# Weight blocks split in halves, and recurrence steps emitted once per weight block, in a projection kernel with three recurrences

## The chip, the cores and the metric

The kernel runs on one core of one Trainium2 chip. The metric is the device time of one execution in microseconds, median of three runs. TensorE (PE) does the matrix products, VectorE (DVE) and ScalarE (ACT) the elementwise work, GpSimd (POOL) some copies and fills, and SyncE (SP) issues the loads.

## The reference

A layer over 272 tokens (16 meta tokens and 256 real ones) with a model width of 2048, in float32. The tokens are normalised and multiplied by one wide matrix; the columns of the result feed three recurrent mixers (A, B and C), three gates, and two outer products:

```python
xn = rmsnorm(h, norm_g[l])
(a_q, a_f, a_i, a_z, b_q, b_k, b_v, b_o, b_ig, b_fg, b_z,
 c_r, c_k, c_v, c_wd, c_ad, c_z, g_a, g_b, g_c) = split_cols(xn @ w_in[l])
y_a = hgrn2_mixer(...)      # A: 8 heads of 128
y_b = mlstm_mixer(...)      # B: 4 heads of 128 x 256
y_c = rwkv7_mixer(...)      # C: 16 heads of 64, with a triangular solve per chunk of 64
merged = (jax.nn.sigmoid(g_a) * (y_a @ w_br[l, 0])
          + jax.nn.sigmoid(g_b) * (y_b @ w_br[l, 1])
          + jax.nn.sigmoid(g_c) * (y_c @ w_br[l, 2]))
h = h + merged @ w_out[l]
return rmsnorm(h, final_norm_g)[:, N_META:]
```

Each mixer is a recurrence over chunks of the sequence: elementwise work, small products, and a state that one chunk hands to the next.

## The kernel before

**Products.** Weights and activations are split into a high and a low part (`wh` and `wl`, `xH` and `xL`), and each product of the reference becomes three: high by high, low by high, high by low. The weights stream from memory in blocks of 512 KB: four pieces of 128 rows by 256 columns in the projections, two of 128 by 512 in the gates and the last product. `Stream.load` (line 343) sends a block to one of four `raw` buffers through SP's queue. `Stream.cut` (line 351) makes its two parts: one ACT cast of the whole block gives `wh`, and one DVE subtraction of the whole block gives `wl`; both have three buffers. `Stream.next` (line 367) hands out the oldest cut block and cuts ahead, so that three are ready or on the way.

**Projections.** `gemm` (line 390) makes 256 columns of the wide matrix at a time, from four blocks. In each block `unit` does 12 products for the first 128 columns and 12 for the second: 24 products per block. Results are read out of PSUM by `evac` when all four blocks are done.

**Recurrences beside them.** Each mixer's work for a group of heads is a generator (`c_scan`, `b_scan`, `a_scan`) that emits a few instructions and yields. `Order` decides how far each generator runs: it keeps a clock for PE, ACT and DVE and adds a price per instruction (for DVE 0.07 us and 1.05 ns per element, for ACT 0.12 us and 0.84 ns). `Order.pump` (line 87) runs every generator whose next step is ready by these clocks within a look-ahead: 3.5 us for a step without a product; for one that starts with a product 2.0 us in C's scans and 0.3 us in B's and A's. `gemm` calls `pump` after each `unit`, so after every 12 products; `rows_unit` (line 1347), for the gates, calls it after every third product of 512 columns. `Order.finish` (line 105) runs a generator to its end at once; it is called where the next group needs the place of the last one (C's at the next R projection, B's at the next head, A's at the next group). The framework then fixes the order of each engine's instructions at build time. The engines run them in that order.

**Stages.** To 38 us the tokens are normalised and transposed and the first columns made. To 717 us follow 47 projections with the recurrences of C (four groups), B (four heads) and A (four groups) beside them. Then come three gate branches (`gate_branch`) and the product with `w_out`. `x_again` (line 1415), after the last gate of the first branch, opens the pool `rows` and writes `late["rp"]`; by then all recurrences are over.

C's scan holds the longest chains: a substitution of 31 steps on DVE (`Ltmp` and `LV`, two instructions each), scratch transfers through memory (`scv`, `sct`, `Vm`, `VT`), and then five chunks with three dependent products each (`cX`, `UV`, `cS`).

Of the kernel before, what the change touches and what calls it, by code (L numbers as in the profile page):

```python
# [9 lines left out]
F32 = mybir.dt.float32  # L10
# [4 lines left out]
ALU = mybir.AluOpType  # L15
# [135 lines left out]
def kernel(  # L151
# [29 lines left out]
    od = Order()  # L181
    V = Priced(nc.vector, "dve", od, tc)
    S = Priced(nc.scalar, "act", od, tc)
# [148 lines left out]
    class Stream:  # L332
# [18 lines left out]
        def cut(self):  # L351
            if not self.raw:
                return
            raw, uk, m = self.raw.pop(0)
            if self.extra and len(self.todo) + len(self.raw) < len(self.extra):
                h, l = self.extra.pop(0)
            else:
                h = wts.tile([P, uk, max(m, 256)], F32R, name="wh", tag="wh", bufs=3)
                l = wts.tile([P, uk, max(m, 256)], F32R, name="wl", tag="wl", bufs=3)
            saved, od.ready = od.ready, 0.0  # L360
            S.copy(out=h[:, :, 0:m], in_=raw[:, :, 0:m])
            od.ready = 0.0
            V.tensor_tensor(out=l[:, :, 0:m], in0=raw[:, :, 0:m], in1=h[:, :, 0:m].bitcast(F32), op=ALU.subtract)
            od.ready = saved
            self.split.append((h, l))

        def next(self):
# [4 lines left out]
                self.load()  # L372
            return self.split.pop(0)

    ws = Stream()

    def unit(h, l, u, kts, ps, aH, aL, t0, n, js):
        for k in range(UK):
            kk = u * UK + k
            rh = aH[:, kk, t0:t0 + n]  # L380
            mm(ps, h[:, k, js], rh, start=kk == 0, stop=False)
            mm(ps, h[:, k, js], aL[:, kk, t0:t0 + n], start=False, stop=False)
            mm(ps, l[:, k, js], rh, start=False, stop=kk == kts - 1)

    def apart(f):
        saved, od.ready = od.ready, od.clk["pe"]
        f()
        od.ready = saved

    def gemm(m, aH, aL, kts, t0, n, evac):  # L390
        nt = m // P
        ps = [gps.tile([P, 512], F32, name="gp", tag="g") for _ in range(nt)]
        for u in range(kts // UK):
            h, l = ws.next()
            for j in range(nt):
                unit(h, l, u, kts, ps[j][:, 0:n], aH, aL, t0, n, slice(j * P, (j + 1) * P))
                od.pump()
        for j in range(nt):
            apart(lambda: evac(j, ps[j][:, 0:n]))

# [2 lines left out]
    def proj(c0, m, t0, evac, before=None, after=None):  # L403
        ws_src = win[:, :, c0:c0 + m]
        blocks.append((ws_src, KT, lambda: gemm(m, xH, xL, KT, t0, T - t0, evac), before, after))
# [927 lines left out]

    late = {}
    WB = 512
    TK = 2

# [222 lines left out]
    for u in range(KT // UK):  # L1562
        h, l = ws.next()
        unit(h, l, u, KT, gw[0][:, 0:T], xH, xL, 0, T, slice(0, P))
        h, l = ws.next()
# [103 lines left out]
    for n, (c0, m) in enumerate(outs):  # L1669
        ps = [gps.tile([P, 512], F32, name="gp", tag="g") for _ in range(2)]  # L1670
        us = KT * m // 1024
        if n < len(outs) - 1:
            for u in range(us):
                h, l = ws.next()
# [55 lines left out]
```

## Time and profile before

| | |
|---|---|
| median of 3 runs | 1229.77 us (1229.72 to 1230.2) |
| profiled execution, its own time | 1229.33 us |
| span of its instructions | 1227.6 us |
| granted TensorE clock | 0.998 |
| PE busy | 1208.1 us (98%) |
| DVE busy | 879.2 us (72%) |
| ACT busy | 665.0 us (54%) |

The span runs from the first to the last instruction of the program; 1.7 us of the profiled execution's time lie around it. Busy time of an engine is the time in which at least one of its instructions ran, and a PE that is busy to 98% may still be late in single places: products overlap by more than half of their modelled length, so the lost time is read from the distance of their starts.

### The profile page before, as it was taken

What the parts mean: (1) busy time and instruction counts of PE and PEld (TensorE: products, weight loads), DVE (VectorE), ACT (ScalarE), POOL (GpSimd) and SP (SyncE); (2) the same over time, 40 slices, a digit from 0 to 9 for tenths busy, and PEclk for the clock granted to TensorE, in tenths of its full rate; (3) what the DMA queues carried; (4) which work ended last, traced back from release to release, by engine and by line L of the source; (5) the groups of instructions that cost most, each with busy time, mean ns of one, the idle gap of its engine ahead of it and who ended that gap; (6) DMA issues with size and microseconds to landing.
All of it is one profiled execution on the core that took longest, in us unless ns stands there. A gap on an engine that the chain in (4) does not pass through costs nothing.

```text
span 1227.6 us, 23061 instructions
## 1 busy us (share of the span) xinstructions
PE 1208.1 (98%) x9224; PEld 1104.2 (90%) x9224; DVE 879.2 (72%) x1491; ACT 665.0 (54%) x1032; POOL 57.0 (5%) x167
## 2 busy tenths in 40 slices
PE   8999999999999999999999999999999999999997
PEld 8999999999999999999999988888888888888887
DVE  6688996697975889995889986644555565556554
ACT  6765455663445764766664657544444444445444
POOL 3100001000051000010000000000000000000000
PEclk9999999999999999999999999999999999999999
DMA  8645564465563554463554454666766676665663
GB/s 254 184 138 166 155 172 130 129 183 155 155 171 104 158 165 137 140 170 105 162 163 142 139 164 153 190 188 189 226 197 193 191 225 200 191 193 172 193 197 121
DMA packets 172996, 207.43 MB, mean 169 GB/s; under 512 B 22331, under 2 KB 127160, under 8 KB 172488
## 3 DMA queue, kind: packets, MB, share of 16 engines
q1 hardware_dynamic: 171688, 202.21, 56.2%
q0 software_dynamic: 880, 3.22, 0.8%
q8 instruction: 72, 1.18, 0.4%
q10 hardware_dynamic: 320, 0.53, 0.1%
q14 instruction: 36, 0.29, 0.1%
HBM read 202.19 MB, written 3.74 MB: 168 GB/s over the span
## 4 chain that ended last, share of the span: by engine, by line
PE 85%; DVE 9%; ACT 3%; issue 2%; POOL 0%; DVEq 0%; ACTq 0%; POOLq 0%
PE gp L186 76%; PE cbank L186 5%; DVE wl L127 3%; PE bank L186 3%; ACT wh L127 1%; DVE Ltmp L127 1%; PE cbank L193 1%; DVE LV L127 1%; PE bank L193 1%; DVE UV L127 0%; DVE aY L127 0%; ACT L127 0%; DVE BK L127 0%; DVE aW L127 0%; DVE SC L127 0%
## 5 line engine op out<-in xcount | busy, mean ns | idle before, releaser
L127 DVE TENSOR_TENSOR wl<-raw,wh 128x1024 fp32r<-128x1024 f32 (+1 forms) x370 | 449.3, 1215 | 243.6 <-ACT wh L127 242.2
L127 ACT CAST wh<-raw 128x1024 fp32r<-128x1024 f32 (+1 forms) x370 | 386.7, 1046 | 387.0 <-PE gp L186 352.4
L186 PE MATMUL gp<-xH,wh 128*128 128x272 f32 (+3 forms) x1552 | 448.1, 289 | 0.2 <-ACT xH L127 0.2
L186 PE MATMUL gp<-xH,wl 128*128 128x272 f32 (+3 forms) x1552 | 444.0, 286 | 1.6 <-DVE wl L127 1.6
L186 PE MATMUL gp<-xL,wh 128*128 128x272 f32 (+3 forms) x1552 | 443.8, 286 | 0.1
L186 PEld LDWEIGHTS gp<-xH,wl 128*128 128x128 f32 x1552 | 292.4, 188 | 2.9 <-DVE wl L127 2.6
L186 PEld LDWEIGHTS gp<-xH,wh 128*128 128x128 f32 x1552 | 292.5, 188 | 2.2 <-ACT xH L127 0.5
L186 PEld LDWEIGHTS gp<-xL,wh 128*128 128x128 f32 x1552 | 292.2, 188 | 0.9 <-DVE xL L127 0.3
L186 PE MATMUL gp<-wh,xH 128*128 128x512 f32 x384 | 150.6, 392 | 0.0
L186 PE MATMUL gp<-wh,xL 128*128 128x512 f32 x384 | 150.5, 392 | 0.0
L186 PE MATMUL gp<-wl,xH 128*128 128x512 f32 x384 | 150.3, 391 | 0.0
L186 PEld LDWEIGHTS gp<-wh,xL 128*128 128x128 f32 x384 | 72.1, 188 | 15.5
L186 PEld LDWEIGHTS gp<-wl,xH 128*128 128x128 f32 x384 | 72.2, 188 | 15.0
L186 PEld LDWEIGHTS gp<-wh,xH 128*128 128x128 f32 x384 | 72.1, 188 | 15.0
L186 PE MATMUL gp<-wh,mH 128*128 128x512 f32 (+1 forms) x144 | 51.1, 355 | 0.0
L186 PE MATMUL gp<-wh,mL 128*128 128x512 f32 (+1 forms) x144 | 50.9, 354 | 0.0
L186 PE MATMUL gp<-wl,mH 128*128 128x512 f32 (+1 forms) x144 | 50.9, 354 | 0.0
L127 DVE TENSOR_TENSOR LV<-LV,Ltmp 40x31 f32<-40x31 f32 (+15 forms) x124 | 41.0, 331 | 2.6
L127 DVE TENSOR_TENSOR Ltmp<-LU,LV 40x31 f32<-40x31 f32 (+15 forms) x124 | 41.1, 332 | 2.4
L186 PEld LDWEIGHTS gp<-wh,mL 128*128 128x128 f32 x144 | 27.2, 189 | 3.8
L186 PEld LDWEIGHTS gp<-wh,mH 128*128 128x128 f32 x144 | 27.2, 189 | 3.7
L186 PEld LDWEIGHTS gp<-wl,mH 128*128 128x128 f32 x144 | 27.2, 189 | 3.7
(420 smaller groups left out, 1476.0 us busy)
## 6 DMA issues: line engine op xcount, KB each, us to landing
raw<-in_w_in_dram SPq DMA_DIRECT2D x288, 512.0 KB, 3.7
raw<-in_w_br_dram SPq DMA_DIRECT2D x48, 512.0 KB, 4.2
raw<-in_w_out_dram SPq DMA_DIRECT2D x32, 512.0 KB, 3.6
hres<-in_x_dram POOLq DMA_DIRECT2D x2, 1024.0 KB, 5.9
xt<-in_x_dram SPq DMA_DIRECT2D x3, 512.0 KB, 5.0
raw<-in_w_in_dram SPq DMA_DIRECT2D x4, 256.0 KB
fg<-in_final_norm_g_dram POOLq DMA_DIRECT2D x1, 1024.0 KB, 5.1
scr<-SC SPq DMA_DIRECT2D x16, 40.0 KB, 1.7
```

The source lines that it names most:

```text
L127: r = f(*a, **k)
L186: nc.tensor.matmul(o, lhsT, rhs, start=start, stop=stop)
L193: nc.tensor.transpose(o, a, i)
```

## The change

A block of full size (1024 elements per partition) is cut in two halves of 512, each with its own ACT cast and its own DVE subtraction, until `late["rp"]` exists; smaller blocks, and those after it, are cut whole. In `gemm`, `pump` is called after both units of a block, so after 24 products and no longer after 12. `late = {}` stands earlier in the file, as `cut` reads it.

```diff
             saved, od.ready = od.ready, 0.0
-            S.copy(out=h[:, :, 0:m], in_=raw[:, :, 0:m])
-            od.ready = 0.0
-            V.tensor_tensor(out=l[:, :, 0:m], in0=raw[:, :, 0:m], in1=h[:, :, 0:m].bitcast(F32), op=ALU.subtract)
+
+            n = 1 if uk * m < 1024 or "rp" in late else 2
+            for i in range(n):
+                us = slice(i * uk // n, (i + 1) * uk // n)
+                od.ready = 0.0
+                S.copy(out=h[:, us, 0:m], in_=raw[:, us, 0:m])
+                od.ready = 0.0
+                V.tensor_tensor(out=l[:, us, 0:m], in0=raw[:, us, 0:m], in1=h[:, us, 0:m].bitcast(F32), op=ALU.subtract)
             od.ready = saved
             self.split.append((h, l))
...
+    late = {}
     ws = Stream()
...
             h, l = ws.next()
             for j in range(nt):
                 unit(h, l, u, kts, ps[j][:, 0:n], aH, aL, t0, n, slice(j * P, (j + 1) * P))
-                od.pump()
+            od.pump()
...
-    late = {}
     WB = 512
```

## Rows read from the trace of the kernel before

**Rows 1.** Head of the page: span, busy time of each engine.

```profile
span 1227.6 us, 23061 instructions
...
PE 1208.1 (98%) x9224; PEld 1104.2 (90%) x9224; DVE 879.2 (72%) x1491; ACT 665.0 (54%) x1032; POOL 57.0 (5%) x167
```

**Rows 2.** Busy time by window: the four substitutions summed, and the gates.

```profile
sum 224.50, PE 220.59 PEld 217.57 DVE 217.49 ACT 120.30 POOL 1.55; mean PE 55.15 PEld 54.39 DVE 54.37 ACT 30.07 POOL 0.39
...
764.00:1116.00 352.00, 352.00 (x1549) 290.30 (x1548) 189.39 (x185) 156.06 (x165) 1.07 (x2) 1.00 0.66 200
```

**Rows 3.** Waits of PE, 30 to 762 us: total, times, longest.

```profile
PE bank L186 <- DVE aW L127: 1.6, 2, 1.0
PE gp L186 <- DVE wl L127: 1.6, 4, 0.7
PE cbank L186 <- DVE SC L127: 1.5, 4, 0.6
PE bank L186 <- DVE aYL L127: 1.1, 2, 0.8
PE cbank L186 <- ACT cX L127: 0.9, 3, 0.3
PE cbank L186 <- DVE UV L127: 0.5, 1, 0.5
```

**Rows 4.** PE's timeline at two waits: start, length, instruction, idle before.

```profile
519.67 0.28 PE L186 MATMUL gp<-xL,wh 128*128 128x256 f32 x1
520.39 0.39 PE L186 MATMUL gp<-xH,wl 128*128 128x256 f32 x1 [0.44 <-DVE wl L127]
...
701.43 0.39 PE L186 MATMUL gp<-xH,wl 128*128 128x256 f32 x1 [0.73 <-DVE wl L127]
```

**Rows 5.** PE's timeline where products resume after a recurrence step.

```profile
409.77 0.38 PE L186 MATMUL gp<-xH,wh 128*128 128x256 f32 x1
409.99 0.28 PE L186 MATMUL gp<-xL,wh 128*128 128x256 f32 x1
```

**Rows 6.** Instruction groups by form: whole blocks and small blocks, cast and subtraction.

```profile
L127 ACT CAST wh<-raw 128x1024 fp32r<-128x1024 f32 x366 | 384.3, 1050 | 387.0 <-PE gp L186 352.4 <-issue 22.3 <-DVE bdn L127 2.9
...
L127 ACT CAST wh<-raw 128x512 fp32r<-128x512 f32 x4 | 2.5, 626 | 0.0
...
L127 DVE TENSOR_TENSOR wl<-raw,wh 128x1024 fp32r<-128x1024 f32 x366 | 446.6, 1221 | 243.5 <-ACT wh L127 242.1
...
L127 DVE TENSOR_TENSOR wl<-raw,wh 128x512 fp32r<-128x512 f32 x4 | 2.8, 688 | 0.2 <-ACT wh L127 0.2
```

**Rows 7.** DVE's timeline: what runs ahead of three instructions that PE awaits.

```profile
275.62 1.22 DVE L127 TENSOR_TENSOR wl<-raw,wh 128x1024 fp32r<-128x1024 f32 x1
276.75 1.41 DVE L127 TENSOR_TENSOR SC<-cbank,cmask 128x256 f32<-128x256 f32 x4
...
519.12 1.21 DVE L127 TENSOR_TENSOR wl<-raw,wh 128x1024 fp32r<-128x1024 f32 x1
...
656.02 1.21 DVE L127 TENSOR_TENSOR wl<-raw,wh 128x1024 fp32r<-128x1024 f32 x1
```

**Rows 8.** DVE's timeline: an instruction that needs nothing of the last one.

```profile
176.61 1.21 DVE L127 TENSOR_TENSOR wl<-raw,wh 128x1024 fp32r<-128x1024 f32 x1
177.74 0.23 DVE L127 TENSOR_TENSOR Ltmp<-LU,LV 40x87 f32<-40x87 f32 x1
```

**Rows 9.** The four substitution windows, instructions on `wl` alone, summed.

```profile
sum 224.50, PE 149.56 PEld 99.06 DVE 76.49; mean PE 37.39 PEld 24.76 DVE 19.12
```

**Rows 10.** The chain that ended last: stretches of products between steps, start and length.

```profile
121.62 1.38 PE gp L186 x12
...
709.91 1.42 PE gp L186 x12
...
374.74 1.08 PE gp L186 x9
```

**Rows 11.** Waits of SP's queue, whole span: total, times, longest.

```profile
SPq L348 <- DVE wl L127: 689.5, 268, 7.7
```

## The prediction, made before the change was run

> **What bounds the kernel now.** I read the head of the page first. PE is busy for 1208.1 of 1227.6 us [rows 1], so the kernel is bound by PE's own products, and a change that adds or removes no product can move only what PE loses between them. The windows by stage come second. In the four stretches in which C's substitution runs (224.5 us together) DVE is busy for 217.5 us, which leaves it 7.0 us; in the gates (764 to 1116 us) it is busy for 189.4 of 352 us and PE never stops [rows 2]. So whatever is to be won or lost lies before 762 us, and in the substitutions DVE is as full as PE.
>
> Third come PE's waits from 30 to 762 us. The six largest make 7.2 us in 16 waits, and nearly all end with a DVE instruction: 1.6 us for `wl` itself in four waits, 5.6 us for recurrence steps in twelve (`aW`, `SC`, `aYL`, `cX`, `UV`) [rows 3]. A wait costs more than its idle time, because the end of a product is modelled: from 519.67 to 520.39 us two starts lie 0.72 us apart, where undisturbed products start 0.12 us apart (12 of them in 1.38 us [rows 10]), so 0.60 us are lost where 0.44 are written [rows 4]. I add 0.16 us per wait: 2.2 us lost on `wl`, 7.5 us on the steps, 9.7 us in all. The fourth view is what DVE did just before. At 275.62 a whole `wl` subtraction of 1.22 us stands directly ahead of the `SC` products, at 656.02 one stands ahead of `aW`, and at 519.12 the subtraction that PE awaits began too late, behind other work [rows 7]. One instruction of 1.2 us at the wrong moment is the pattern. Last, when products resume after a step, the first one takes 0.22 us (409.77 to 409.99) instead of 0.12: 0.10 us per interruption [rows 5].
>
> **The change part by part.**
>
> *Halves, price.* The blocks cut in two are the 192 of the start and the projections, and some 47 in the first gate branch. The sizes are in the trace, since four small blocks have 512 elements: 688 ns on DVE against 1221, 626 ns on ACT against 1050 [rows 6]. Two halves thus take 2 x 688 - 1221 = 155 ns more on DVE, and 2 x 626 - 1050 = 202 ns on ACT, if each waits for the end of the last. They need not: the instruction after a subtraction starts at 177.74, 0.08 us before that one's end at 177.82 [rows 8]. With one such overlap inside the pair the price is about 75 ns on DVE, and with a like one some 0.12 us on ACT (an estimate from the same rows). The four substitution windows hold 76.5 / 1.221 = 63 subtractions [rows 9]: 63 x 0.075 = 4.7 us of more DVE work, at most 63 x 0.155 = 9.8, against the 7.0 us that are free there. ACT is busy for 120 of the 224.5 us in them [rows 2], so its 63 x 0.12 = 7.6 us are hidden; without that cover they would be added to the same chain. The 47 cuts in the gates (47 x 0.155 = 7.3 us at most) are hidden by DVE's 163 free us there and would cost those 7.3 if the gates were DVE's. In the start, four blocks are cut while PE waits for its first columns: 4 x 0.075 = 0.3 us at most, 0 at least; I take 0.1. Of the 4.7 us I let 1.1 reach PE, as DVE has a little room but it does not lie evenly. Bounds 0 and 9.8; the sum carries +1.2 for both.
>
> *Halves, gain on `wl`.* PE's first products on `wl` need the first two of the block's four pieces. They wait for 688 instead of 1221 ns: 0.53 us less. The two waits shown lose 0.60 and 0.73 + 0.16 = 0.89 us [rows 4], so the other two share 0.7 of the 2.2; -0.53, -0.53 and twice -0.35 make -1.8. Bounds 0 (both halves run behind each other before PE is told) and -2.2.
>
> *Halves, gain on steps.* For the twelve waits on recurrence steps, the best case is that the awaited instruction goes between the halves: 12 x 0.53 = 6.4 us less. The worst is that both halves stay ahead of it: 12 x 0.075 = 0.9 more. What follows the first half is decided by what is ready, and the steps of one block are emitted behind cuts made earlier and ahead of the next ones, so both orders will occur. I take the middle, -3.0.
>
> *Pump per block.* Between two calls of `next` nothing else is emitted, so a step that moves from the first to the second pump of a block passes no cut and no `load`: on DVE, ACT, SP and POOL it keeps its neighbours, and its DMAs (`scr`, `LU`, `scv`, `sct`, `Vm`, `VT`) and POOL's fills and copies stand where they stood between the same loads. SP's queue waits for `wl` nearly always [rows 11], and now for the second half: 0.155 us later at most, against four `raw` buffers. What moves is the step's PE part, by up to 12 products, about 1.4 us [rows 10]. That makes a result more likely to be there when PE comes to it, and joins some interruptions. In the list of the chain, ten stretches outside C's forced chains have exactly 12 products between two steps (first and last shown) [rows 10]; if all ten pairs join, 10 x 0.10 = 1.0 us is saved, and none if each pair moves on by a block. I take -1.0, since a pump can no longer stop after 12. In C's five chunks nothing moves: `finish` has emitted them already, and the stretches of 9 products there [rows 10] show that the build orders them by readiness.
>
> *Sum.* +1.2 - 1.8 - 3.0 - 1.0 = -4.6 us. The profiled execution took 1229.33 us, so 1224.7; the median of the runs stands 0.44 higher, so 1225.2 us.
>
> **The rivals.**
>
> *Hidden anyway (no change).* The order of instructions is made anew, and what `SC` or `aW` gain, another step loses, as PE is 98% busy [rows 1] and each wait is short. Only the `wl` gain is certain in kind: 1229.8 - 1.8 = 1228.0 us. For it: the build orders PE by readiness [rows 10], so the pump's place may decide little. Against: the same kind of instruction stands ahead of wait after wait [rows 7].
>
> *DVE becomes the bound (slower).* Place: the four substitutions. The planner books 0.07 us for the second half's start; the trace's pair costs up to 0.155, so 0.085 us per cut is not planned for, and DVE falls behind by 63 x 0.085 = 5.4 us over the four windows. At their ends `wl` is late already (519.12, and the wait at 701.43). With the `wl` gain left, 1229.8 + 5.4 - 1.8 = 1233.4 us. It decides once the unabsorbed price per cut passes what the halves give per cut, (1.8 + 3.0) / 63 = 0.076 us. For it: 7.0 free us in 224.5 [rows 2]. Against: the overlap of 0.08 us [rows 8] brings the price to 0.075. The Trainium skill, "VectorE: DVE Perf Modes", section "The TRN2 errata", says that every instruction which reads SBUF pays a fixed extra latency, large tiles once and small ones each time, and advises 512 elements or more; the halves stand at that limit. Its section "The DRAIN you can't avoid" has the next instruction start only when the pipe is empty, with an exception for one that is not held; by the rule without the exception the pair would cost its full 0.155 us and this rival would hold. The row at 177.74 is such an exception, and only the halves' own trace can show on which side they fall.
>
> *Steps side by side (slower).* With one pump per block, two dependent steps of C's scan can fall into one pump (look-ahead 2.0 us) with no products between them. `SC` waits 0.6 us already with 12 products ahead of it [rows 3]; without them it would wait 1.4 us more. Four groups with one such pair each, 5.6 us: 1229.8 + 5.6 - 1.8 = 1233.6 us. Against: the build can put products between, as in the chunks [rows 10].
>
> **How the numbers follow.** Under 0.2% (2.5 us) a difference can't be told from none in this kernel. The forecast has 0.52: its price is small, and four views point at the same cause. Hidden anyway has 0.26, DVE as the bound 0.14, steps side by side 0.08. So faster 0.52, same 0.26, slower 0.22. The forecast's own range is 1221 (the steps' best case, -6.4 instead of -3.0, and nothing lost on DVE) to 1227.3, where it turns into no change. The range for 8 in 10 goes from 1221.0 to 1233.0 us: it holds the forecast, the hidden case and the nearer part of the two slower ones.
>
> **What would show it.** Right: subtractions of 512 elements near 690 ns with starts 0.6 us apart, PE's waits for `wl` near zero, those for `SC`, `aW` and `aYL` about halved, stretches of products in multiples of 24 outside the chunks, and windows in which the substitution ends no more than 1 us later. Wrong: DVE without a free microsecond in the substitutions and longer waits of PE at their ends (DVE as the bound); new waits between C's products (steps side by side); or waits as many and as long, only for other instructions (hidden anyway).

## The result and the profile after

The change makes the kernel slower. It takes 1249.55 us (median, 1247.11 to 1252.24), the kernel before 1229.74 us beside it: a ratio of 1.0164, 95% interval 1.0137 to 1.0190. The forecast was 1225.2 us, with 1233.0 as the upper end of its range. The profiled execution after took 1247.9 us, with a span of 1246.2 us, 18.6 more than before [rows 1]. Its page, head and clock by slice:

```profile
span 1246.2 us, 23535 instructions
...
PE 1214.6 (97%) x9224; PEld 1108.9 (89%) x9224; DVE 889.7 (71%) x1729; ACT 684.2 (55%) x1270; POOL 55.7 (4%) x167
...
PE   8999999999999999999999996999999999999997
...
PEclk9999999999999999999999996999999999999999
```

PE has the same 9224 products. DVE gained 10.5 us in 1246 and is no fuller than before. The page shows one bad slice out of 40, the 25th (748 to 779 us); there PE is busy to six tenths and its granted clock falls as well. Busy time by window says how local the loss is. Each line has the window and its length, the busy time and the number of instructions of PE, PEld (PE's weight loads), DVE, ACT and POOL, the granted clock, and the DMA's share and GB/s. First the kernel before, up to its 6371st product and from its first gate product to its first branch product (the first with `yHB`):

```profile
0.00:691.73 691.73, 681.55 (x6371) 663.47 (x6372) 569.77 (x1114) 408.93 (x703) 51.79 (x156) 1.00 0.55 156
715.30:754.00 38.70, 37.97 (x421) 30.01 (x419) 26.00 (x58) 24.56 (x58) 3.60 (x8) 1.00 0.37 110
```

and the same stretches after, the second also in its late part, and the first products of the branch:

```profile
0.00:690.93 690.93, 680.81 (x6371) 661.85 (x6372) 570.00 (x1279) 422.99 (x890) 51.68 (x156) 1.00 0.55 156
713.20:772.70 59.50, 47.05 (x541) 38.33 (x540) 39.79 (x104) 32.16 (x78) 2.37 (x8) 0.86 0.37 107
740.60:772.70 32.10, 21.28 (x237) 18.16 (x236) 14.50 (x36) 18.50 (x51) 2.37 (x8) 0.75 0.16 49
772.70:782.00 9.30, 9.30 (x33) 7.47 (x33) 5.99 (x10) 5.77 (x10) 0.57 (x1) 0.77 0.41 129
```

After the same 6371 products the changed kernel is 0.8 us ahead (690.93 against 691.73). DVE's time up to there is the same, although the halves cost DVE more, because most of the last substitution is still to come (its tiles are below). From there to the first branch product it needs 81.8 us and not 62.3: the whole loss, 18.7 us at that product (772.7 against 754.0), arises in some 80 us. What is late there shows when the tiles of C's last group are followed. Each line has the shortest, median and longest duration in ns, then the first and the last start in us. The lines are the substitution's `Ltmp` in the first, third and last group, the chunks' `cX` in the last, and the read-out of the first gate, `sg`. Before:

```profile
L127 DVE TENSOR_TENSOR Ltmp<-LU,LV x31: 184/349/418, 124.1 to 178.8; 40x31 f32<-40x31 f32 x2, 40x60 f32<-40x60 f32 x2, 40x87 f32<-40x87 f32 x2, 40x112 f32<-40x112 f32 x2
L127 DVE TENSOR_TENSOR Ltmp<-LU,LV x31: 179/351/417, 461.6 to 520.3; 40x31 f32<-40x31 f32 x2, 40x60 f32<-40x60 f32 x2, 40x87 f32<-40x87 f32 x2, 40x112 f32<-40x112 f32 x2
L127 DVE TENSOR_TENSOR Ltmp<-LU,LV x31: 172/352/420, 642.4 to 701.3; 40x31 f32<-40x31 f32 x2, 40x60 f32<-40x60 f32 x2, 40x87 f32<-40x87 f32 x2, 40x112 f32<-40x112 f32 x2
L127 DVE COPY cX<-cbank x5: 278/283/284, 720.6 to 744.0; 64x128 f32<-64x128 f32 x5
L127 ACT ACTIVATE sg<-gp x2: 605/624/644, 753.2 to 755.0; 128x512 f32<-128x512 f32 x2
```

After, the same five:

```profile
L127 DVE TENSOR_TENSOR Ltmp<-LU,LV x31: 175/349/418, 134.7 to 191.4; 40x31 f32<-40x31 f32 x2, 40x60 f32<-40x60 f32 x2, 40x87 f32<-40x87 f32 x2, 40x112 f32<-40x112 f32 x2
L127 DVE TENSOR_TENSOR Ltmp<-LU,LV x31: 172/349/416, 467.9 to 534.8; 40x31 f32<-40x31 f32 x2, 40x60 f32<-40x60 f32 x2, 40x87 f32<-40x87 f32 x2, 40x112 f32<-40x112 f32 x2
L127 DVE TENSOR_TENSOR Ltmp<-LU,LV x31: 174/351/418, 673.9 to 723.4; 40x31 f32<-40x31 f32 x2, 40x60 f32<-40x60 f32 x2, 40x87 f32<-40x87 f32 x2, 40x112 f32<-40x112 f32 x2
L127 DVE COPY cX<-cbank x5: 282/283/283, 742.8 to 765.2; 64x128 f32<-64x128 f32 x5
L127 ACT ACTIVATE sg<-gp x2: 577/587/597, 769.1 to 770.7; 128x512 f32<-128x512 f32 x2
```

The first group's substitution starts 10.6 us later than before and ends 12.6 later, the third ends 14.5 later, and neither costs anything, since 691 us are reached on time. The last one ends 22.1 us later, and `cX` starts 22.2 us later. That is when PE runs dry. PE's timeline at the last product of the first gate, and where products start again:

```profile
740.12 0.39 PE L186 MATMUL gp<-wh,xH 128*128 128x512 f32 x1
740.35 0.40 PE L186 MATMUL gp<-wl,xH 128*128 128x512 f32 x1
740.58 0.40 PE L186 MATMUL gp<-wh,xL 128*128 128x512 f32 x1
740.94 0.65 PE L186 MATMUL cbank<-Vm,ZT 32*32 32x32 f32 x28
...
771.70 0.55 PE L186 MATMUL cbank<-cSL,bonesR 128*128 128x256 f32 x1 [2.92 <-DVE cSL L127]
...
772.68 0.63 PE L186 MATMUL gp<-wh,yHB 128*128 128x512 f32 x1
773.11 0.63 PE L186 MATMUL gp<-wl,yHB 128*128 128x512 f32 x1
```

Between 740.6 and 772.7 there is no weight product at all. `l_setup` finishes C's scan and closes its pool before `sg` exists, so the first gate's 96 products are the last that can run beside C's chain; the gate is read out at 769.1 (before: 753.2) and the branch follows. That the closing of the pool holds the branch back is read from the code and from this order of starts; no run moved it. Inside that stretch PE waits for C's own steps, one after the other (us in total, times, longest):

```profile
PE cbank L186 <- ACT UV L127: 4.3, 6, 1.2
PE cbank L186 <- DVE cSL L127: 2.9, 1, 2.9
PE cbank L186 <- ACT cX L127: 2.2, 3, 0.7
PE cbank L186 <- DVE UV L127: 1.4, 1, 1.4
```

That is 10.8 us of idle time; a wait of 1.5 us for `wl` stands ahead of it, inside the first gate. The rest of the loss is the clock (starts 0.43 us apart at 772.68, where they were 0.23 apart at 740.12) and 120 more recurrence products between gate and branch (541 against 421 in the windows above). All 120 are A's: 104 of 32 columns that before ran ahead of the gate, and 16 that before ran behind the first branch product. No run separates these two.

### The profile page after: what moved, and what is told of

Same layout as the page of the kernel before. It is cut to its first block, busy times and chain, and to the rows that moved or that the text cites. A ratio compares the mean times of both kernels' runs of the same rounds, so it can differ in the third digit from the quotient of the medians.

```text
span 1246.2 us, 23535 instructions
## 1 busy us (share of the span) xinstructions
PE 1214.6 (97%) x9224; PEld 1108.9 (89%) x9224; DVE 889.7 (71%) x1729; ACT 684.2 (55%) x1270; POOL 55.7 (4%) x167
## 4 chain that ended last, share of the span: by engine, by line
PE 87%; DVE 9%; ACT 2%; issue 1%; DMA 1%; SPq 0%; ACTq 0%; DVEq 0%
PE gp L186 78%; PE cbank L186 5%; PE bank L186 2%; DVE wl L127 2%; PE cbank L193 1%; DVE LV L127 1%; DVE Ltmp L127 1%; ACT wh L127 1%; PE bank L193 1%; DMA xt<-in_x_dram 1%; DVE aM L127 0%; DVE aW L127 0%; DVE aY L127 0%; DVE aMM L127 0%; DVE UV L127 0%
## 5 line engine op out<-in xcount | busy, mean ns | idle before, releaser
L127 DVE TENSOR_TENSOR wl<-raw,wh 128x512 fp32r<-128x512 f32 (+1 forms) x608 | 472.4, 797 | 244.0 <-ACT wh L127 238.8
L127 ACT CAST wh<-raw 128x512 fp32r<-128x512 f32 (+1 forms) x608 | 413.9, 709 | 390.2 <-PE gp L186 353.6
```

The source lines that it names most:

```text
L127: r = f(*a, **k)
```

## The experiments

Two theories to begin with. **Theory P, pace:** the loss comes from *when* C's steps are emitted. `pump` lets a step go only if its inputs are ready within 3.5 us of PE's clock in the planner, while DVE's and ACT's clocks may stand up to `CAP` = 5 us ahead of PE's. So a scan that has just booked a long DVE step is stopped until PE's clock has moved on, and goes on at the next pump. Half as many pumps make it late by a little at step after step, and a higher price of a cut does the same. **Theory D, DVE:** the second halves' real work on DVE delays the chain. Ratios are to the kernel before on the same chip, with 95% intervals.

**e1: halves alone** (`cut` as changed, `od.pump()` after each unit).

```diff
-            od.pump()
+                od.pump()
```

> Kernel before with the halves alone, pump after every 12 products as before. Theory P (the rarer pump slows C's recurrence, and at the first gate PE runs out of independent products): this run stays near the kernel before, 1225 to 1233 us, with at most a few microseconds lost between the first gate product and the first product of the first branch (38.7 us before, 60 us in the changed kernel). Theory D (the halves overload DVE): this run carries most of the loss, 1243 us or more.

Measured: 1237.13 us, 1.0062 (1.0050 to 1.0075). Both theories missed: the halves alone already cost 7.7 us.

**e2: one pump per block alone** (cuts whole).

> Kernel before with the pump after 24 products alone, blocks cut whole. Theory P: most of the loss is here, 1240 to 1250 us, C's last substitution starts some 25 to 30 us later than before (642 us) and ends after 718 us, and PE idles some 15 us or more between 735 and 775 us. Theory D: 1225 to 1232 us.

Measured: 1242.95 us, 1.0110 (1.0096 to 1.0124), with not one more instruction on DVE. The time is as P said, and D can't explain it. The last group's tiles come as late as in the whole change:

```profile
L127 DVE TENSOR_TENSOR Ltmp<-LU,LV x31: 169/349/406, 672.7 to 723.0; 40x31 f32<-40x31 f32 x2, 40x60 f32<-40x60 f32 x2, 40x87 f32<-40x87 f32 x2, 40x112 f32<-40x112 f32 x2
L127 DVE COPY cX<-cbank x5: 282/283/284, 740.4 to 762.2; 64x128 f32<-64x128 f32 x5
```

The substitution starts 30.3 us later than before, and its last step starts at 723.0, about as P had it. P's idle time was too high: PE is idle for 10.5 of the 40 us from 735 to 775, and not for 15 or more.

**e3: the change with a longer look-ahead, and e4: the kernel before with a shorter one.**

```diff
-    AHEAD = 3.5
+    AHEAD = 6.0
```

> The changed kernel with the planner's look-ahead for steps without a product raised from 3.5 to 6.0 us, nothing else. Theory P says the loss comes from one step per pump, as the planner's DVE and ACT clocks run up to 5 us ahead of PE's and 3.5 us lets one step pass; 6.0 lets several pass, so the recurrence regains its pace and the time falls to 1222 to 1233 us, with C's last substitution over by about 705 us. Theory D: the DVE work is the same, so 1243 us or more stays.

> The kernel before with the look-ahead for steps without a product lowered from 3.5 to 2.0 us: whole cuts, pump after 12 products. Theory P: the pace of C's steps falls without either edit of the change, the last group's chain comes late again, 1236 to 1248 us, with PE idle between 735 and 775 us. Theory D: no change, 1227 to 1233 us.

Measured: e3 1231.64 us, 1.0019 (1.0010 to 1.0028); e4 (`AHEAD = 2.0`) 1240.80 us, 1.0090 (1.0075 to 1.0106). One constant of the planner takes back 18 of the 20 us, with every half and every missing pump still there, and brings 11 us of loss into the kernel before. That pace is the main cause is shown; the tiles of e3's last group are back near those of before:

```profile
L127 DVE TENSOR_TENSOR Ltmp<-LU,LV x31: 172/349/419, 645.5 to 703.8; 40x31 f32<-40x31 f32 x2, 40x60 f32<-40x60 f32 x2, 40x87 f32<-40x87 f32 x2, 40x112 f32<-40x112 f32 x2
L127 DVE COPY cX<-cbank x5: 273/282/284, 724.2 to 745.7; 64x128 f32<-64x128 f32 x5
```

**e5: halves, booked at the old price.** e1 left open whether its 7.7 us are real work or the planner's price. To e1's kernel this is added:

```diff
+            clk = dict(od.clk)
+            for e, c in (("act", 0.12 + 0.84e-3 * uk * m), ("dve", 0.07 + 1.05e-3 * uk * m)):
+                clk[e] = max(clk[e], 0.0, od.clk["pe"] - 3.0) + c
             for i in range(n):
...
+            od.clk.update(clk)
```

> Halves as in the change, pump after every 12 products as before, but the planner books a cut at the price of one whole block, so that every recurrence step is emitted at the same place as in the kernel before. Halves alone cost 7.7 us (1237.1 us). Theory of the price: these came from the planner, which held the steps back because it booked 0.07 us on DVE and 0.12 us on ACT more per cut; with the old price the time falls to 1225 to 1230 us and the first product of the first branch starts no later than 38 to 40 us after the first gate product. Theory of real work: the second half's start-up on DVE is what costs, and it is still there; the time stays at 1235 to 1239 us.

Measured: 1226.28 us, 0.9981 (0.9972 to 0.9990). The same halves that cost 7.7 us in e1 gain 2.7 us once the planner books them as before. In e1 it was the price.

**e6 and e7: one pump per block in some blocks only** (whole cuts).

```diff
+            ws.done += 1
...
-                od.pump()
+                if ws.done > 104 or j == nt - 1:
+                    od.pump()
```

> Whole cuts; one pump per block in the first 104 of the 192 blocks of the projections (through C's first two groups and most of the way to the third), after that one pump per 12 products as before, so that C's last group is emitted in the same blocks as in the kernel before. One pump per block everywhere cost 13.5 us (1243.0 us). Theory of the last group: a late step costs only where no projection is left to cover it, so nothing is lost here: 1225 to 1230 us. Theory of a toll on every block (each block with one pump loses a little): 104 / 192 of 13.5 us, so 1236 to 1238 us.

> The converse with far fewer blocks: whole cuts, two pumps per block as before up to block 160, one per block only in the last 32 of the 192, while C's last group prepares and runs its substitution. Theory of the last group: 32 blocks do most of the damage, 1236 to 1244 us, with the substitution of the last group ending some 10 us later and the gap between the first gate product and the first branch product above 45 us. Theory of a toll on every block: 32 / 192 of 13.5 us, so 1231 to 1233 us.

Measured: e6 1228.54 us, 0.9998 (0.9990 to 1.0007); e7 (`ws.done <= 160`) 1232.31 us, 1.0030 (1.0019 to 1.0042). e6 excludes an even toll on every block: 104 of 192 blocks, over half, cost nothing. e7 alone would fit the toll's figure (1231 to 1233), and my own was too high: its substitution, which had started on time, ends 8.1 us late and not 10, `cX` comes 7.7 us late, and from gate to branch it takes 42.1 us and not 45. So the last 32 blocks alone do not do most of the damage (3.4 of 13.5 us). As neither run makes the substitution start late, e2's late start should come from the blocks 105 to 160; no run changed these alone. The last group's tiles, e6 and then e7:

```profile
L127 DVE TENSOR_TENSOR Ltmp<-LU,LV x31: 174/350/418, 642.1 to 700.9; 40x31 f32<-40x31 f32 x2, 40x60 f32<-40x60 f32 x2, 40x87 f32<-40x87 f32 x2, 40x112 f32<-40x112 f32 x2
L127 DVE COPY cX<-cbank x5: 277/283/284, 719.9 to 743.3; 64x128 f32<-64x128 f32 x5
```

```profile
L127 DVE TENSOR_TENSOR Ltmp<-LU,LV x31: 172/351/418, 643.6 to 709.4; 40x31 f32<-40x31 f32 x2, 40x60 f32<-40x60 f32 x2, 40x87 f32<-40x87 f32 x2, 40x112 f32<-40x112 f32 x2
L127 DVE COPY cX<-cbank x5: 282/282/284, 728.3 to 748.3; 64x128 f32<-64x128 f32 x5
```

**e8: e5 and e6 together.**

> The halves of e5 (booked as one whole cut) with the pumping of e6. If both theories hold (price in the planner, last group), C's last group is emitted as in the kernel before and the gains of the change are kept: waits for wl gone and joined interruptions, 1223 to 1228 us. If the halves cost real work on DVE, 1235 us or more.

Measured: 1227.15 us, 0.9985 (0.9976 to 0.9994). Faster than both kernels, and no faster than e5: pumping once per block gives nothing even where it does no harm.

**e9 to e11: more projections behind C's last group.** C's last group and A's second change places, so that four projections more stand between it and the gates: in the kernel before (e9), in e2's (e10) and in the changed one (e11).

```diff
-(b_group, 1), (c_group, 2), (a_group, 0), (a_group, 1), (c_group, 3),
+(b_group, 1), (c_group, 2), (a_group, 0), (c_group, 3), (a_group, 1),
```

> The kernel before with one change of order: C's last group changes places with A's second, so that four projections (16 blocks) more lie between it and the gates. It is the base line for the next two. C's third group is finished 16 blocks sooner, so some loss there may be seen, and less at the end: 1225 to 1240 us by every theory. Its difference to the next two is what counts.

> As the last one, with one pump per block in all 192 blocks (whole cuts). Theory of cover (a late step of C's last group costs only because the 96 products of the first gate are all that PE has left): with four projections more behind it the lateness is hidden, and this run is within 4 us of the last one. Theory of pace (one pump per block costs its 13.5 us wherever the groups stand): 10 us or more above the last one.

> The whole change (halves at the planner's full price, one pump per block) in the same order of groups. Theory of cover: of the 20 us that the change costs in the old order nearly all is gone, and the run is from 5 us below to 4 us above that of the kernel before in this order. Theory of pace or of real work on DVE: 10 to 20 us above it.

Measured: 1259.63 (1.0248, 1.0234 to 1.0262), 1258.88 (1.0247, 1.0233 to 1.0261) and 1261.56 us (1.0266, 1.0252 to 1.0280). With cover at the end, one pump per block costs nothing (-0.8 us) and the whole change 1.9 us, where they cost 13.5 and 20. But the new order costs 31 us by itself, and these stand elsewhere. The windows of e9, from 504 to 600 us and from gate to branch:

```profile
504.00:600.00 96.00, 80.00 (x706) 75.43 (x705) 60.57 (x112) 55.47 (x106) 5.07 (x12) 0.86 0.37 108
757.70:782.40 24.70, 24.70 (x275) 19.89 (x274) 19.89 (x38) 12.13 (x17) 0.00 (x0) 1.00 0.53 175
```

Between gate and branch PE never stops now. Instead it is idle for 16.0 of the 96 us from 504 to 600 (before: 1.9 of them), where C's *third* group is finished 16 blocks early. The window of the kernel before, and PE's largest wait in e9:

```profile
504.00:600.00 96.00, 94.06 (x1039) 90.02 (x1038) 76.25 (x147) 64.01 (x120) 4.69 (x11) 1.00 0.48 135
```

```profile
PE gp L186 <- DVE cK L127: 6.3, 1, 6.3
```

`cK` is the read-out of a projection, and PE's next one can't start without it. It looks like the same loss at another group: `finish` forces a chain out, and other work stands behind it; no run shows that. That e9 to e11 are alike is therefore weaker evidence than e6, as all three share that larger loss, with a granted clock of 0.86 in it.

**e12 to e14: what is left between the change and e2.** e12 is the whole change with e5's price. e13 is e12 with whole cuts from the first gate on, e14 the converse; their edits follow in this order.

```diff
-            n = 1 if uk * m < 1024 or "rp" in late else 2
+            n = 1 if uk * m < 1024 or "lp" in late else 2
```

```diff
-            n = 1 if uk * m < 1024 or "rp" in late else 2
+            n = 2 if uk * m == 1024 and "lp" in late and "rp" not in late else 1
```

> The whole change (halves, one pump per block), with the planner booking a cut at the price of one whole block; every recurrence step is then emitted in the same block as with one pump per block and whole cuts (1243.0 us). Theory of the price: the 6.6 us by which the change stands above that kernel come from the planner's dearer halves, and they go: 1238 to 1243 us (halves at the old price gained 2.6 us when nothing else was changed). Theory of work: with the substitution of the last group late already, the second halves lengthen it on DVE, and the run stays at 1246 to 1251 us.

> The change with the old price booked, as in the run before (1248.0 us), but blocks cut after the first gate has begun are cut whole: halves in the projections, none beside C's late last chunks. Theory of the late chain: the 5 us above the kernel with whole cuts and one pump per block (1243.0 us) come from second halves that stand ahead of cX, UV and cS on ACT and DVE while PE waits for them, so they go: 1241 to 1244.5 us. Theory of the projections: the halves lengthen the way to the chain (the substitution), and the run stays at 1246 to 1250 us.

> The converse: whole cuts in the projections, halves only from the beginning of the first gate to the end of the first branch, one pump per block, old price booked. Theory of the late chain: 1246 to 1250 us. Theory of the projections: 1241 to 1244.5 us.

Measured: e12 1247.97 us, 1.0155 (1.0141 to 1.0169); e13 1248.90 us, 1.0170 (1.0155 to 1.0184); e14 1244.10 us, 1.0121 (1.0108 to 1.0135). The price theory that held in e1 falls here: the old price takes back 1.2 us of 6.3 (each run against its own kernel before), and the times of the executions overlap. A likely reason, not shown, is that with one pump per block the steps wait for the block's end in any case. My next theory, that the second halves stand in the way of C's late chunks, falls with e13. It is halves in the *projections* that add 5 to 6 us when the chain is late (e13 against e14 and e2). Why is not settled. `cX` can't carry it: it starts 1.0 us later in e13 than in e2 (table below). Part of it is scatter: e13's profiled execution (1246.2 us, its fastest) stands 2.5 us above e2's (1243.8 us, its slowest). What the runs show beside it is the clock: e13's five executions took 1246.2, 1247.7, 1248.9, 1251.3 and 1252.0 us at mean granted clocks of 0.991, 0.989, 0.989, 0.986 and 0.985, while e2's and e14's stand at 0.990 to 0.992 and within 1.7 us of each other.

All runs in the old order of groups, by the start of `cX` in C's last group (us, profiled execution):

| kernel | first `cX` | first branch product | median | against before |
|---|---|---|---|---|
| e5, halves at the old price | 718.0 | 751.4 | 1226.28 | -2.7 |
| e8, e5 with e6 | 719.1 | 752.5 | 1227.15 | -1.8 |
| e6, per block until 104 | 719.9 | 753.3 | 1228.54 | -0.4 |
| before | 720.6 | 754.0 | 1229.74 | |
| e3, change with AHEAD 6 | 724.2 | 755.7 | 1231.64 | +2.2 |
| e7, per block from 160 | 728.3 | 755.2 | 1232.31 | +3.4 |
| e1, halves | 735.6 | 762.9 | 1237.13 | +7.7 |
| e4, before with AHEAD 2 | 736.4 | 767.1 | 1240.80 | +11.4 |
| e14, halves in the gates | 738.9 | 769.0 | 1244.10 | +15.1 |
| e2, per block | 740.4 | 769.7 | 1242.95 | +13.5 |
| e12, change at the old price | 740.9 | 771.4 | 1247.97 | +18.6 |
| e13, halves before the gates | 741.4 | 772.5 | 1248.90 | +19.9 |
| the change | 742.8 | 772.7 | 1249.55 | +19.8 |

Whatever moved `cX`, the time follows it by and large, but not in proportion: 7.7 us of lateness cost 3.4 (e7), 15.0 cost 7.7 (e1), and the change's 22.2 cost 19.8. Between 738 and 743 us it is no longer a guide (e14, e2, e12 and e13, as said). The third column is the better one: from the first branch product to the end the profiled executions take 473.7 to 477.0 us in all 13 kernels, so nearly the whole difference is there when the branch starts. The gate's products cover the first part of the lateness; what nothing covers is paid, and the clock comes on top.

## Why the prediction was wrong, step by step

*Pump per block* is the step that failed. It said that a step "that moves from the first to the second pump of a block passes no cut and no `load`", that only its PE part moves, by up to 12 products, and that "in C's five chunks nothing moves". That is right for one step and wrong for a chain. A scan's next step is released only at a later pump, so what one step loses the next did not win back: the substitution of C's last group came to start 31.5 us later (30.3 in e2). `finish` does emit the chunks in the same place, but their inputs came 22 us late, when the gate's products were used up. I costed the step at -1.0; alone it measures +13.5 (e2). With it falls the premise that the change "can move only what PE loses between them": 9.7 us were counted as lost before, and the change added 10.8 us of new idle time in one place. The rival *Steps side by side* was near in kind (C's steps with no products between them), but it put them into single pumps, at 5.6 us, and not at the end.

*Halves, price.* The size on the chip was right. DVE's timeline has two halves in 1.29 us, and the groups by form have the mean [rows 6]:

```profile
142.43 1.29 DVE L127 TENSOR_TENSOR wl<-raw,wh 128x512 fp32r<-128x512 f32 x2
```

```profile
L127 DVE TENSOR_TENSOR wl<-raw,wh 128x512 fp32r<-128x512 f32 x480 | 315.8, 684 | 87.6 <-ACT wh L127 82.4 <-PE bank L186 2.1 <-PE gp L186 1.1
```

1.29 - 1.22 = 0.07 us per cut, where 0.075 was taken; the other pairs that stand alone side by side take 1.25 to 1.29. End to end, two of 0.684 us would take 1.37, so the second half starts before the first is over. The Trainium skill, "VectorE: DVE Perf Modes", section "The DRAIN you can't avoid", lets the next instruction start only when the pipe is empty, with an exception for one that is not held; this pair takes the side of the exception. Wrong was what I did with the planner's price: I used it only to ask whether DVE would fall behind the plan. The plan itself got slower by it, and that was worth 10.4 us in e1 (+7.7 there, -2.7 in e5), far more than the real work shows.

*Halves, gains on `wl` and on steps.* With the pace untouched (e5) the halves gain 2.7 us, where the three terms gave +1.2 - 1.8 - 3.0 = -3.6. (The middle of the two cases for the steps, -6.4 and +0.9, is -2.7; the prediction writes -3.0.) The sum was near, but its parts came out otherwise, so the nearness is in part luck. PE's waits from 30 us to the 6371st product fall by only 0.8 us, from 6.2 to 5.4. Three lines of e5 in that stretch:

```profile
PE cbank L186 <- DVE SC L127: 1.5, 3, 1.0
PE bank L186 <- DVE aW L127: 1.2, 2, 0.7
PE gp L186 <- DVE wl L127: 0.8, 3, 0.3
```

and of the kernel before and the whole change on `wl`, in this order:

```profile
PE gp L186 <- DVE wl L127: 0.6, 2, 0.4
```

```profile
PE gp L186 <- DVE wl L127: 2.0, 2, 1.8
```

The waits for `wl` did not go to zero: there are three where there were two, the longest 0.3 us where it was 0.4, and in the whole change they grew. From 30 to 762 us they are 1.4 us in five in e5, where it was 1.6 in four [rows 3]. Of the steps, `SC` is awaited as long as before, `aW` 0.4 us less, and only the waits for `aYL` (1.1 us [rows 3]) are gone. Where the rest of the 2.7 us comes from is open.

*DVE becomes the bound* did not hold as the main cause: e2, with no work added to DVE, has 13.5 of the 20 us, e5, with all of the halves' work, has none of them, and in the changed kernel the last substitution is shorter than before (49.5 us against 58.9), only later.

*Hidden anyway* holds for the stretch that the sum was made for: up to the 6371st product the change is 0.8 us ahead, though without the gain on `wl`, and one pump per block in 104 blocks gives -0.4 us (e6), which can't be told from none nor from their share of the -1.0.

*What would show it* listed, for the wrong case, new waits between C's products, and these came; it did not list the place, the end of the last group, where nothing is left to hide them.

## What to carry to other kernels

Where a planner interleaves a long dependent chain with other work, how often it is asked, what it is told that an instruction costs, and its look-ahead can set the chain's pace, as all three did here; before changing any of them, follow the chain's last member and ask what still runs beside it when it is late. Here lateness in the middle was free while other work remained, and where that ended it was paid: 22.2 us late cost 19.8. When instructions are split, book the split at the old price first, so that the order stays and the real cost shows, as in e5.

## What the hardware showed that was not expected

The granted clock fell during the stretch without weight products (0.75 over 740.6 to 772.7 us), in which PE ran small products with waits between them. From 760 to 770 us it was 0.50 all through, the lower of its two levels (1.2 GHz; the upper is 2.4). The longest wait of PE that ended in the stretch before 770 was 1.4 us:

```profile
760.00:770.00 10.00, 4.89 (x48) 4.15 (x48) 4.55 (x12) 2.97 (x9) 0.58 (x2) 0.50 0.00 0
```

It came back late: over 772.7 to 782.0, with PE busy throughout, it was still 0.77, and the first branch products started 0.43 us apart, at 1.2 GHz, where those of the gate started 0.23 apart at 2.4 GHz. With the two levels 1 and 0.5, 0.77 of 9.3 us means 4.3 us at the lower one, an estimated 2.1 us of products lost after the wait itself was over; the starts agree, as they are 0.43 us apart until 776.95 and 0.23 from 777.24 on. The mean clock of the profiled execution fell from 0.998 to 0.988, and the changed kernel's executions scatter by 5 us where those of the kernel before scatter by 2.
